# One branch for an expert pair's gate and up products, and one for the two halves of its down product

## The chip, the cores and the metric

The kernel runs on one core of a Trainium2 chip. The metric is the time of one execution on the device in microseconds, the median of the runs; the profile shows one execution, instruction by instruction.

## The reference, cut to what matters

The program computes two stacks of two layers each on 256 tokens of width 1024. The second stack ends each layer with a mixture of 16 experts, and the change lies in these two calls:

```python
def grouped_moe(h, router_w, router_b, w_gate, w_up, w_down):
    # sigmoid router: the best of 4 groups, then the top 2 experts in it
    ...
    for e in range(N_EXPERTS):
        he = jax.nn.silu(t @ w_gate[e]) * (t @ w_up[e])
        y = y + combine[:, e:e + 1] * (he @ w_down[e]).astype(jnp.float32)
```

All of it is float32. An expert has 512 hidden columns, so its gate, up and down weights are 2 MB each.

## The kernel before, in words

`moe` gathers tokens by expert. Experts p and p + 8 form pair p, and the pair shares 128 token slots. How the slots are split between the two is known only at run time: 64 and 64, 96 and 32, or 32 and 96. `gi` holds the split of each pair as 2, 3 or 1, and TensorE loads it into a register (`reg`).

A product of a pair is then written three times, one arm for each split (`products`, L1852 to L1871). `SEG` says how an arm cuts the 128 slots: arm 2 makes two float32 products of 64 columns for each slice of the contraction, arms 3 and 1 make four of 32 columns. `tc.If(gr_ == 2)` (L1865) takes arm 2 or goes on to the inner branch (L1868), which takes arm 3 or arm 1. The arms lie behind one another in TensorE's program: arm 2, arm 3, arm 1, and then the code that follows. So arm 2 jumps over arms 3 and 1 when it ends, arm 3 jumps over arm 1, and arm 1 is reached by two jumps ahead of it. Everything in a branch is scheduled as a unit.

For each of the eight pairs of a call, `pair` (L1873 on) does this on TensorE:

- `products` for the gate (`pg`, 8 slices of the contraction) and `products` for up (`pu`, 8 slices): two branches.
- `gather` (`ga`, L1828): the first half of the next pair's tokens; meanwhile ScalarE takes silu of `pg` (L1879) and VectorE multiplies it by `pu` (L1880).
- four transposes (`tr`, L1886), the second half of `gather`, and then `down(0)` and `down(1)`: two branches of 4 slices each (`pd`), each followed by ScalarE (L1898) and VectorE (L1899), which take the product out of PSUM.
- `back` (`py`, L1906): the rows go back to their tokens, two halves, with `places` (`pw`) for the next pair between them.

In the last pair of a call, `down(1)` is cut in two, with `back(0)` and `back(1)` between the parts, so it has five branches. After the eighth pair stands a loop (L1961) for tokens that found no slot; it ran zero times here.

The weights come in pieces of 1 MB (`piece`, L1620 and L1623, issued by SyncE), 12 for a pair, into a ring of 20 buffers. A piece can be loaded as soon as TensorE has done with the one that held its buffer, 20 pieces earlier.

Of the kernel before, what the change touches and what calls it, by code (L numbers as in the profile page):

```python
# [7 lines left out]
F32 = mybir.dt.float32  # L8
F32R = mybir.dt.float32r
I32 = mybir.dt.int32  # L10
AF = mybir.ActivationFunctionType
OP = mybir.AluOpType
# [5 lines left out]
KD = 8  # L18
# [107 lines left out]
def build(tc, I, out, dump=None, upto=99):  # L126
    nc = tc.nc
    coff, ctot = _const_layout()
    with ExitStack() as ctx:
# [7 lines left out]
        V, S, PE = nc.vector, nc.scalar, nc.tensor  # L137
        mm = PE.matmul
# [31 lines left out]
        def psum(name="ps"):  # L170
            return ps_pool.tile([128, 512], F32, name=name, tag="ps")
# [81 lines left out]
        def mod_buf():  # L253
            return mw["pool"].tile([128, 2048], F32, name="modw", tag="modw", bufs=2)
# [36 lines left out]
        def mod_first(w, b0, bias, dst, dst2, bufs, ahead_=None):  # L291

            rs = []
            for i, buf in enumerate(bufs):
                if i == 3 and ahead_:
                    ahead_()
                r = buf.rearrange("p (k c) -> p k c", k=2)
                nc.sync.dma_start(r, w[i * 256:(i + 1) * 256, b0 * 128:(b0 + 8) * 128].rearrange("(k p) c -> p k c", p=128))
                rs.append(r)
            yield  # L300
            p = psum("modp")
            for k in range(KD):
                for g in range(4):
                    mm(p[g * 32:(g + 1) * 32, :256], cst[:, 0, k, :], rs[k // 2][:, k % 2, g * 256:(g + 1) * 256],
                       start=k == 0, stop=k == KD - 1, skip_group_check=True)
                if k < KD - 1:
                    yield
            yield from mod_out(p, b0, 8, bias, ((0, dst), (1, dst2)))
# [558 lines left out]
        def four(p):  # L867
            return p.rearrange("p (a b) -> p a b", b=128)
# [36 lines left out]
        with ExitStack() as c1:  # L905
# [5 lines left out]
            for x in xs:  # L911
# [3 lines left out]
            scale = mod_first(wm[0], 8, *wm[1:], [mod_buf(), mod_buf(), b4[:, :2048], b4[:, 2048:]],  # L915
                              lambda: load2(0))
            w2t = big("w13r", [128, 2, 2, KD, 128])

            def load2(t):
                for ab in range(2):  # L920
                    nc.sync.dma_start(w2t[:, t, ab], w13[:, ab * FF + t * 128:ab * FF + (t + 1) * 128]
                                      .rearrange("(k p) c -> p k c", p=128))
# [663 lines left out]
        def moe(l, a, op, pre=None, post=None):  # L1586


            with ExitStack() as c1:
# [6 lines left out]
                todo = [(p, e, nm, hf) for p in range(8) for nm in ("exp_w_gate_2", "exp_w_up_2", "exp_w_down_2")  # L1596
                        for hf in range(2) for e in range(2)]
# [71 lines left out]
                w_, r_ = ([f("ew", [128, 4096], F32) for _ in range(n)] for f, n in ((big2, NW), (big, NR)))  # L1669
# [18 lines left out]
                def tm():  # L1688
                    ring_t.append(ring_t.pop(0))
                    return ring_t[-1]  # L1690
# [8 lines left out]
                for tt in range(2):  # L1699
                    V.scalar_tensor_tensor(sc[:, tt], pm[:, 32 + tt * NE:32 + (tt + 1) * NE], rst[:, tt:tt + 1], srow,  # L1700
                                           op0=OP.mult, op1=OP.add)
# [24 lines left out]
                for o, n, d in ((0, 3, 1), (3, 2, 2), (5, 1, 3)):  # L1726
# [44 lines left out]
                                       op0=OP.add, op1=OP.add)  # L1771
# [6 lines left out]
                xg_b = b0_[:, 2 * D:].rearrange("p (k c) -> p k c", k=KD)  # L1778
# [54 lines left out]
                def places(oh, wcol, b):  # L1833
# [5 lines left out]
                    for tt in range(2):  # L1839
# [8 lines left out]
                SEG = {2: ((0, 64, 0), (64, 64, 1)),  # L1848
                       3: ((0, 32, 0), (32, 32, 0), (64, 32, 0), (96, 32, 1)),
                       1: ((0, 32, 0), (32, 32, 1), (64, 32, 1), (96, 32, 1))}  # L1850

                def products(p, x, n_k, w_, gr_, ks=None):  # L1852


                    def arm(n):
                        for k in ks or range(n_k):
                            ws, kp = w_(k)
                            for o, m, e in SEG[n]:
                                mm(p[o:o + m, :], x[:, k, o:o + m], ws[e][kp], start=k == 0, stop=k == n_k - 1,  # L1859
                                   skip_group_check=True)  # L1860
                    if gr_ is None:
                        arm(2)
                        return
                    with tc.issue_after(last[ENG.PE]):
                        with tc.If(gr_ == 2) as c:  # L1865
                            arm(2)
                        with c.Else():
                            with tc.If(gr_ == 3) as c2:  # L1868
                                arm(3)
                            with c2.Else():  # L1870
                                arm(1)  # L1871

                def pair(pl, w_, gr_, nxt=lambda i: None, last_=False):  # L1873

                    pg, pu = psum("pg"), psum("pu")
                    products(pg, xg_b, KD, lambda k: (w_("exp_w_gate_2", k // 4), k % 4), gr_)
                    products(pu, xg_b, KD, lambda k: (w_("exp_w_up_2", k // 4), k % 4), gr_)
                    act = tm()
                    S.activation(act, pg, AF.Silu)  # L1879
                    V.tensor_mul(act, act, pu)  # L1880
                    sw, ohT = pl
                    nxt(0)
                    hT = four(tm())
                    p = psum("tr")
                    for i in range(4):
                        pin(PE.transpose(p[:, i * 128:(i + 1) * 128], act.rearrange("s (j k) -> s k j", k=4)[:, i], ident))  # L1886
                    V.tensor_copy(hT, four(p))
                    nxt(1)
                    dh, dl = b1_[:, :D], b1_[:, D:2 * D]

                    def down(dd, between=None):
                        pd = psum("pd")
                        cs = slice(dd * 512, (dd + 1) * 512)
                        for ks in (range(0, 2), range(2, 4)) if between else (None,):
                            products(pd, hT, 4, lambda k: (w_("exp_w_down_2", k // 2), k % 2 * 2 + dd), gr_, ks)
                            if between and ks[0] == 0:
                                between()
                        S.activation(dh[:, cs], pd, AF.Copy, scale=sw)  # L1898
                        V.scalar_tensor_tensor(dl[:, cs], pd, sw, dh[:, cs].bitcast(F32), op0=OP.mult, op1=OP.subtract)  # L1899

                    def back(d2):
                        py = psum("py")
                        for d in range(2):
                            k = d2 * 2 + d
                            for i, x in enumerate((dh, dl)):
                                pin(mm(py[:, d * T:(d + 1) * T], x[:, k * 128:(k + 1) * 128], ohT,  # L1906
                                       start=i == 0, stop=i == 1))
                        for d in range(2):
                            k = d2 * 2 + d
                            V.scalar_tensor_tensor(XT[:, k], py[:, d * T:(d + 1) * T], g2[:, k:k + 1], XT[:, k],  # L1910
                                                   op0=OP.mult, op1=OP.add)
                    down(0)

                    def half1():
                        back(0)
                        back(1)
                    down(1, half1) if last_ else (down(1), half1())
                    if pre and last_ and gr_ is not None:
                        next(pre, None)
                    if post and last_:  # L1920
                        post(0, tm())
                        post(1, tm())
                    nxt(2)
                    back(2)
                    back(3)
                    if post and last_:
                        post(2, tm())
                        post(3, tm())
# [8 lines left out]
                for p in range(8):  # L1937
                    def nxt(i):
                        if p == 7:
                            return  # L1940
                        if i == 0:
                            gather(ohs[p + 1], 0)
                        elif i == 1:
                            gather(ohs[p + 1], 4)
                        else:
                            pl[p + 1] = places(ohs[p + 1], wt[:, :, p + 1], (p + 1) % 2)
# [14 lines left out]
                with tc.For_i(0, n_extra, 1) as it:  # L1961
# [44 lines left out]
                    def w_(nm, hf):  # L2006
                        if (nm, hf) not in got:
                            b = 2 * len(got)
                            got[nm, hf] = [piece(bufs[2 + (b + e) % 6], I[nm][l][bass.ds(pr_ + 8 * e, 1)]
                                                 .rearrange("o a b -> (o a) b"), nm, hf) for e in range(2)]  # L2010
                        return got[nm, hf]
# [52 lines left out]
```

## Time and profile before

| what | value |
|---|---|
| median of 3 runs | 2053.97 us (2050.93 to 2060.8) |
| profiled execution | 2052.47 us, span 2050.7 us |
| TensorE busy | 1945.3 us, 95% of the span, 14344 matmul records |
| mean granted TensorE clock | 0.979 |
| first call of `moe`, first gate product to last return | 1411.8 to 1639.5 us |
| second call | 1807.5 to 2042 us |

A float32 product appears as two matmul records with a weight load each. PE is TensorE's matmul row, PEld its weight loads, PEldq the instructions that its sequencer handles by itself, such as a branch. The sequencer runs ahead of the array and fills a queue, so a branch stands in the trace before the products ahead of it have run. In the timeline, the number in brackets is how long the engine sat idle before the row. "issue" is a wait for nothing that the profile shows. The queue q8 carries instructions, q1 data.

### The profile page before, as it was taken

To read this page: it belongs to the slowest core of one execution; us is meant where nothing else is said; L and a number is where in the kernel's file an instruction comes from. 1 tells how busy PE (TensorE), PEld (TensorE's weight loads), DVE (VectorE), ACT (ScalarE), POOL (GpSimd) and SP (SyncE) were. 2 spreads that over 40 slices of the span, in tenths; PEclk is the share of its full clock that TensorE was granted. 3 is DMA by queue.
4 is the path that set the end of the run, shared out by engine and by line. 5 is a ranking of instruction groups with operands and counts; after the bars stand their busy time and mean duration, and the time that the engine had idled before them with its cause. 6 is when DMAs were issued, how large, how long until landed. Compare 5 with 4: busy or idle time off the path is not lost. (4 is left out here: it accounts for less than half of the span.)

```text
span 2050.7 us, 34453 instructions
## 1 busy us (share of the span) xinstructions
PE 1945.3 (95%) x14344; PEld 1599.1 (78%) x14344; DVE 1286.9 (63%) x2188; ACT 734.0 (36%) x1075; POOL 64.6 (3%) x60
## 2 busy tenths in 40 slices
PE   6999999999899999999999999998999889889997
PEld 5889899888699989999999999975444488744443
DVE  6357677858797959796798777853223287533222
ACT  4322222245454444445654445441000167500001
POOL 0000000011010010001010010000000010000000
PEclk8999999999999999999999999999999999989999
DMA  8678697734396869776486946468999544879992
GB/s 296 241 252 297 245 325 270 258 103 124 104 335 216 301 172 321 254 261 236 165 299 210 317 150 218 156 233 327 412 416 413 216 149 145 339 321 416 416 411 90
DMA packets 240525, 534.76 MB, mean 261 GB/s; under 512 B 13132, under 2 KB 168128, under 8 KB 206528
## 3 DMA queue, kind: packets, MB, share of 16 engines
q1 hardware_dynamic: 237424, 531.54, 72.0%
q8 instruction: 162, 2.65, 0.5%
q10 hardware_dynamic: 2896, 0.21, 0.2%
q14 instruction: 43, 0.35, 0.0%
HBM read 530.65 MB, written 1.07 MB: 259 GB/s over the span
## 5 line engine op out<-in xcount | busy, mean ns | idle before, releaser
L448 PE MATMUL pa<-hh,whl 128*128 128x258 f32 (+1 forms) x880 | 252.4, 287 | 3.6 <-ACT hh L516 3.6
L450 PE MATMUL pa<-hh,whl 128*128 128x258 f32 (+1 forms) x880 | 249.5, 283 | 4.9 <-DVE whl L419 4.9
L449 PE MATMUL pa<-hl,whl 128*128 128x258 f32 (+1 forms) x880 | 249.4, 283 | 3.3 <-DVE hl L517 3.3
L448 PE MATMUL pb<-hh,whl 128*128 128x258 f32 (+1 forms) x880 | 249.3, 283 | 0.8 <-ACT s L564 0.8
L449 PE MATMUL pb<-hl,whl 128*128 128x258 f32 (+1 forms) x880 | 249.0, 283 | 0.0
L450 PE MATMUL pb<-hh,whl 128*128 128x258 f32 (+1 forms) x880 | 248.9, 283 | 0.0
L324 DVE SCALAR_TENSOR_TENSOR macc<-modw,cst,macc 128x1024 f32<-128x1024 f32 (+1 forms) x182 | 219.9, 1235 | 23.0 <-DMA modw<-in_w_mod_dram 16.1
L418 ACT ACTIVATE whl<-w13r 128x2048 fp32r<-128x2048 f32 x88 | 168.5, 1914 | 179.7 <-PE pb L450 86.3
L419 DVE TENSOR_TENSOR whl<-w13r,whl 128x2048 fp32r<-128x2048 f32 x88 | 201.6, 2291 | 38.5 <-ACT whl L418 38.5
L450 PE MATMUL py<-gh,whl 128*128 128x256 f32 (+1 forms) x704 | 216.7, 308 | 2.7 <-DVE whl L419 2.7
L448 PE MATMUL py<-gh,whl 128*128 128x256 f32 (+1 forms) x704 | 218.4, 310 | 0.1
L449 PE MATMUL py<-gl,whl 128*128 128x256 f32 (+1 forms) x704 | 216.3, 307 | 0.0
L448 PE MATMUL lin<-hh,whl 128*128 128x258 f32 x640 | 188.6, 296 | 5.6 <-ACT hh L516 5.6
L449 PE MATMUL lin<-hl,whl 128*128 128x258 f32 x640 | 181.9, 285 | 3.3 <-DVE hl L517 3.3
L450 PE MATMUL lin<-hh,whl 128*128 128x258 f32 x640 | 181.4, 284 | 0.0
L448 PEld LDWEIGHTS pa<-hh,whl 128*128 128x128 f32 x880 | 166.8, 189 | 11.6 <-ACT hh L516 3.8
L450 PEld LDWEIGHTS pa<-hh,whl 128*128 128x128 f32 x880 | 167.3, 190 | 5.7 <-DVE whl L419 5.3
L449 PEld LDWEIGHTS pa<-hl,whl 128*128 128x128 f32 x880 | 167.7, 191 | 4.1 <-DVE hl L517 3.9
L448 PEld LDWEIGHTS pb<-hh,whl 128*128 128x128 f32 x880 | 166.8, 190 | 1.8 <-ACT s L564 1.0
L450 PEld LDWEIGHTS pb<-hh,whl 128*128 128x128 f32 x880 | 166.9, 190 | 0.4 <-issue 0.4
L449 PEld LDWEIGHTS pb<-hl,whl 128*128 128x128 f32 x880 | 166.9, 190 | 0.0
L418 ACT ACTIVATE whl<-w2r 128x768 fp32r<-128x768 f32 (+3 forms) x80 | 90.7, 1143 | 160.4 <-PE py L450 106.2
(444 smaller groups left out, 3766.7 us busy)
## 6 DMA issues: line engine op xcount, KB each, us to landing
w13r<-in_ffn_w_dram SPq DMA_DIRECT2D x86, 1024.0 KB
modw<-in_w_mod_dram SPq DMA_DIRECT2D x62, 1024.0 KB
ew<-in_exp_w_down_dram SPq DMA_DIRECT2D x54, 1024.0 KB
ew<-in_exp_w_gate_dram SPq DMA_DIRECT2D x54, 1024.0 KB
ew<-in_exp_w_up_dram SPq DMA_DIRECT2D x52, 1024.0 KB
modw<-in_ada_w_dram SPq DMA_DIRECT2D x48, 1024.0 KB
w2r<-in_ffn_w_dram SPq DMA_DIRECT2D x18, 1536.0 KB
w2r<-in_ffn_w_dram SPq DMA_DIRECT2D x12, 1280.0 KB
```

The source lines that it names most:

```text
L324: V.scalar_tensor_tensor(acc[h], x, c, acc[h], op0=OP.mult, op1=OP.add)
L418: S.activation(h, src, AF.Copy)
L419: V.tensor_sub(l, src, h.bitcast(F32))
L448: mm(p, ah, bh, start=start, stop=False)
L449: mm(p, ah, bl, start=False, stop=False)
L450: mm(p, al, bh, start=False, stop=stop)
```

## The change

`products` takes a list of products instead of one, and puts all of them into each arm. Gate and up go into one branch, and the two halves of down into another; the last pair of a call keeps three branches for down. Both PSUM tiles of down are made ahead of the branch, and their readers come after it (`out`). A pair that had four branches has two.

```diff
-                def products(p, x, n_k, w_, gr_, ks=None):
+                def products(x, n_k, gr_, todo):
                     def arm(n):
-                        for k in ks or range(n_k):
-                            ws, kp = w_(k)
-                            for o, m, e in SEG[n]:
-                                mm(p[o:o + m, :], x[:, k, o:o + m], ws[e][kp], start=k == 0, stop=k == n_k - 1,
-                                   skip_group_check=True)
+                        for p, w_, ks in todo:
+                            for k in ks or range(n_k):
+                                ws, kp = w_(k)
+                                for o, m, e in SEG[n]:
+                                    mm(p[o:o + m, :], x[:, k, o:o + m], ws[e][kp], start=k == 0, stop=k == n_k - 1,
+                                       skip_group_check=True)
...
-                    products(pg, xg_b, KD, lambda k: (w_("exp_w_gate_2", k // 4), k % 4), gr_)
-                    products(pu, xg_b, KD, lambda k: (w_("exp_w_up_2", k // 4), k % 4), gr_)
+                    products(xg_b, KD, gr_, [(pg, lambda k: (w_("exp_w_gate_2", k // 4), k % 4), None),
+                                             (pu, lambda k: (w_("exp_w_up_2", k // 4), k % 4), None)])
...
-                    def down(dd, between=None):
-                        pd = psum("pd")
+                    pds = [psum("pd") for _ in range(2)]
+                    def down_of(dd, ks=None):
+                        return pds[dd], lambda k: (w_("exp_w_down_2", k // 2), k % 2 * 2 + dd), ks
+                    def out(dd):
                         cs = slice(dd * 512, (dd + 1) * 512)
-                        for ks in (range(0, 2), range(2, 4)) if between else (None,):
-                            products(pd, hT, 4, lambda k: (w_("exp_w_down_2", k // 2), k % 2 * 2 + dd), gr_, ks)
-                            if between and ks[0] == 0:
-                                between()
-                        S.activation(dh[:, cs], pd, AF.Copy, scale=sw)
-                        V.scalar_tensor_tensor(dl[:, cs], pd, sw, dh[:, cs].bitcast(F32), op0=OP.mult, op1=OP.subtract)
+                        S.activation(dh[:, cs], pds[dd], AF.Copy, scale=sw)
+                        V.scalar_tensor_tensor(dl[:, cs], pds[dd], sw, dh[:, cs].bitcast(F32), op0=OP.mult, op1=OP.subtract)
...
-                    down(0)
...
-                    down(1, half1) if last_ else (down(1), half1())
+                    if last_:
+                        products(hT, 4, gr_, [down_of(0)])
+                        out(0)
+                        products(hT, 4, gr_, [down_of(1, range(0, 2))])
+                        half1()
+                        products(hT, 4, gr_, [down_of(1, range(2, 4))])
+                        out(1)
+                    else:
+                        products(hT, 4, gr_, [down_of(0), down_of(1)])
+                        out(0)
+                        out(1)
+                        half1()
```

## Rows read from the trace of the kernel before

**Rows 1.** Busy time by stretch: window, its length, engines, PEclk, DMA share, GB/s.

```profile
1440.00:1468.00 28.00, 28.00 (x157) 13.54 (x158) 8.11 (x19) 1.97 (x3) 0.00 (x0) 1.00 1.01 415
1900.00:1920.00 20.00, 17.73 (x148) 7.72 (x144) 3.01 (x5) 1.28 (x2) 0.00 (x0) 0.91 1.02 412
```

**Rows 2.** Chain that ended last, second pair of the second call: start, us, what.

```profile
1837.09 7.07 PE pg L1859 x63
1844.16 6.87 PE pu L1859 x64
1851.02 1.98 PE ga L1828 x16
...
1853.48 1.79 PE ga L1828 x16
1855.27 7.00 PE pd L1859 x64
```

**Rows 3.** Timeline, TensorE's idle times inside the pairs, both calls.

```profile
1511.43 2.02 PE L1828 MATMUL ga<-oh,nx 128*128 128x128 f32 x16 [1.66 <-DVE tm L1880]
...
1596.99 1.27 PE L1828 MATMUL ga<-oh,nx 128*128 128x128 f32 x10 [1.82 <-issue]
...
1618.88 1.51 PE L1859 MATMUL pu<-ew,nx 128*64 128x512 f32 x6 [0.91 <-PE pg L1859]
...
1837.09 0.63 PE L1859 MATMUL pg<-ew,nx 128*32 128x512 f32 x4 [0.85 <-issue]
...
1903.95 4.48 PE L1859 MATMUL pu<-ew,nx 128*32 128x512 f32 x24 [2.27 <-issue]
...
1968.57 1.16 PE L1828 MATMUL ga<-oh,nx 128*128 128x128 f32 x9 [1.45 <-issue]
...
1991.42 1.08 PE L1859 MATMUL pu<-ew,nx 128*64 128x512 f32 x4 [1.95 <-issue]
```

**Rows 4.** Branches of L1865: duration ns min/median/max; all, then single ones.

```profile
L1865 PEldq COMPARE_BRANCH  x116: 63/188/6082, 1411.2 to 2034.3; - x116
...
L1865 PEldq COMPARE_BRANCH  x1: 5932/5932/5932, 1505.3 to 1505.3; - x1
...
L1865 PEldq COMPARE_BRANCH  x1: 5042/5042/5042, 1613.5 to 1613.5; - x1
...
L1865 PEldq COMPARE_BRANCH  x1: 6082/6082/6082, 1985.0 to 1985.0; - x1
...
L1865 PEldq COMPARE_BRANCH  x1: 2897/2897/2897, 1994.0 to 1994.0; - x1
```

**Rows 5.** DMA queues of the whole span: the instruction queue, packets, MB, share.

```profile
q8 instruction: 162, 2.65, 0.5%
```

**Rows 6.** DMA queues: instructions, 1411.8 to 1637 (first call); all queues, 1636 to 1643.

```profile
q8 instruction: 34, 0.56, 1.0%
...
DMA packets 1, 0.02 MB, mean 2 GB/s; under 512 B 0, under 2 KB 0, under 8 KB 0
```

**Rows 7.** The branch over the loop, end of the first call.

```profile
L1961 PEldq COMPARE_BRANCH  x1: 3325/3325/3325, 1639.7 to 1639.7; - x1
```

**Rows 8.** Gate products: all of them; in the timeline one in arm 2, one in arm 1.

```profile
L1859 PE MATMUL pg<-ew,nx x640: 589/592/643, 1411.8 to 2019.0; 128*64 128x512 f32 x96, 128*32 128x512 f32 x64
...
1411.83 7.09 PE L1859 MATMUL pg<-ew,nx 128*64 128x512 f32 x32
...
1807.50 7.07 PE L1859 MATMUL pg<-ew,nx 128*32 128x512 f32 x64
```

**Rows 9.** A branch of L1865 ahead of a gate product in arm 1.

```profile
L1865 PEldq COMPARE_BRANCH  x1: 207/207/207, 1834.6 to 1834.6; - x1
```

**Rows 10.** Weight issues after the first gate products; busy time after the last weights.

```profile
1415.51 4.24 SPq L1623 DMA_DIRECT2D ew<-in_exp_w_down_dram  x4
...
1812.89 2.70 SPq L1623 DMA_DIRECT2D ew<-in_exp_w_down_dram  x4
...
2012.00:2028.00 16.00, 15.14 (x73) 5.38 (x71) 3.59 (x10) 0.60 (x1) 0.00 (x0) 1.00 0.01 3
```

## The prediction

> **What bounds the kernel now.** I read the profile from the whole to the one pair: busy time by stretch, the chain that ended last, TensorE's idle times, the branches, the instruction queue, and last the weights. [...] The chain runs through TensorE without a break: 7.1 us gate, 6.9 up, 2.0 and 1.8 gather, 7.0 down [rows 2]. Between gate and up, and between the halves of down, where branches stand, no idle time shows here. So what a branch costs has to be looked for in the seven places where TensorE stood: 1.66 + 1.82 + 0.91 + 0.85 + 2.27 + 1.45 + 1.95 = 10.9 us over both calls [rows 3]. Three of the seven stand ahead of or inside a gather, which reads no weights.
>
> The branches explain them. Their median is 0.19 us, but single ones last 5.9, 5.0 and 6.1 us [rows 4], and TensorE's 1.66, 0.91 and 1.95 us of idle time follow these three. The long ones wait for code. The instruction queue brings 162 packets of 2.65 MB / 162 = 16.4 KB [rows 5]. A pair's code, counted from the kernel, is 3 x (64 + 128 + 128) = 960 loads and matmuls of products (gate, up, down; an arm 2 of gate is 32 matmuls, so 64 instructions, an arm 1 twice that [rows 8]), and about 150 for the rest: some 1,110. The first call's eight pairs brought 34 packets [rows 6], so a packet holds about 8 x 1,110 / 34 = 260 instructions; I call it a block and count with 256. All arms are fetched, run or not.
>
> Three things follow from the rows.
>
> - One block ahead is held, not two. The branch over the loop at 1639.7 us skips more than a block and took 3.3 us [rows 7], and the only DMA packet from 1636 to 1643, 0.02 MB, is one of code [rows 6]: the data queues were at rest.
> - In a pair, with the DMA engines full, a block is usable 5.8 us after the sequencer entered the one before: it got out of the 6.08 us branch at 1985.0 + 6.1 = 1991.1, and out of the next long one at 1994.0 + 2.9 = 1996.9 [rows 4].
> - TensorE's queue hides about 4.2 us of such a wait in arm 2: 5.93 - 1.66 = 4.3, 5.04 - 0.91 = 4.1, 6.08 - 1.95 = 4.1 [rows 3, 4].
>
> [...]
>
> **The change part by part.** What it removes is small: two branches of four in 14 pairs and one of five in the last pair of each call, at 0.2 us of sequencer time each [rows 4], all under the queue: 0. Code shrinks by about 8 of 1,110 instructions a pair, so about as many blocks are fetched. What matters is how far a branch now jumps. Arm 2 of gate skipped 256 instructions, one block, and landed in the block that was already asked for. Arm 2 of gate and up together skips 512, two blocks, so the target is never the block at hand.
>
> (a) Gate and up in arm 2. The 640 gate matmuls are 12 x 32 + 4 x 64 [rows 8]: 12 of 16 pairs take arm 2 (all of the first call, four of the second); the other four go through two branches ahead of the arm and none behind it, so arm 1. In the last pair of each call the data queues are at rest and the wait is about the 3.3 us of [rows 7], less than the queue hides. The other 10 wait 5.85 and hide 4.2: 10 x 1.65 = 16.5 us. In the first pair of the first call the sequencer crosses into a block some 20 instructions, 2 us, before the arm ends, and if skipped blocks are fetched in order, a second wait is added: 0 to 5.8 - 2 = 3.8, I take 2.
>
> (b) Behind the landing the queue is empty and the next block has only been asked for. If fewer than about 90 instructions are left in the landing block, TensorE runs them (32 of a gather take 1.98 us, 0.062 each [rows 2]) and stands again. The stop at 1596.99, after one load and one product of the gather [rows 3], fixes a block's edge. Counted from it, with 8 instructions less for each pair, the seven landings of the first call leave 229, 148, 78, 8, 194, 124 and 54 instructions, and the three of the second 178, 108 and 38. The short ones give 5.8 - 0.062 x n = 1.0 + 5.3 + 2.5 + 3.4 = 12.2 us. (An edge that is 50 places off gives 8 to 16.)
>
> (c) Down. The merged branch jumps 256 as one gate branch does now, and lands in the next block. Some will wait as these did, 0.9 to 1.95 us [rows 3]: three of 14 at 1.5, 4.5 us; bounds 0 and 14 x 1.95 = 27.
>
> (d) Arm 1, four pairs. Its jumps lie ahead of the arm: 128 + 256 instructions, 1.5 blocks instead of 0.75. By the same count three of the four land two blocks on. The branch stands at 1834.6 [rows 9] and the product follows about 1 us later (1.5 us less a gap of 0.85 in this pair [rows 3]), so only 1 us is hidden: 4.8 us twice, 2.5 for the first pair, whose data queues are at rest, and 1 for the fourth: 13 us. Bounds: 0, and 4 x 5.8 = 23.
>
> (e) The clock. [...] After 1.95 us, four matmuls took 1.08 [rows 3], full speed. Six of the new gaps are longer than 2.27 us: 6 x 1.7 = 10 us. Bounds 0 and 20.
>
> (f) What stands now, 10.9 and 1.7 us, is replaced: -12.6.
>
> At nothing I cost the readers. ScalarE's silu of `pg` may start only when up is done, if the branch signals at its end: 0.6 us more ahead of the multiplication, under the 2.0 us of gather [rows 2]; without a gather, in two last pairs, 1.2 us. The first half of down is taken out later; that lies under the second half's 3.5 us. If it waited for the branch's end, about 1.5 us would be bare in 14 pairs, 21 us. What I see speaks against it: the signals lie inside an arm, since the first weight issue of a gate came 3.7 us after its start in arm 2 and 5.4 in arm 1, before the 7.1 were over [rows 8, 10]. In arm 1 the gate's buffers come free some 3.5 us later when both share a branch. Behind that wait, on SyncE's queue, stand only weights that are not yet due: from 2012 to 2028 us the data queues move nothing (share 0.01) [rows 10], so the last pieces are ready over 16 us early.
>
> Sum: 16.5 + 2 + 12.2 + 4.5 + 13 + 10 - 12.6 = 45.6 us. Against the profiled execution's own 2052.47 us that is 2098 us; the median of the runs is 1.5 us above it, less than anything here can tell.
>
> **The rivals.** *The long jump is free, faster.* If TensorE holds more than two blocks, or fetches the target while the arm runs, twice as long an arm gives twice the time to do so, and with half the branches the present stalls go: 2052.5 - 10.9 - 1.7 = 2040 us. It decides from a wait under 4.2 us in (a), for then (b) starts with code at hand. For it: most branches of L1865 are short, 0.19 us in the median [rows 4]. Against it: the 3.3 us of [rows 7], where two blocks on was not there although the code before it had run for some microseconds. [...]
>
> *The queue hides it, no change.* Behind 13.7 us of matmuls the queue is always full, so (a) costs 10 x 0 to 0.5 us, and if (b) and (d) are half of what I count, without slow clocks, they take the place of the old 12.6: 2052 to 2062, within 10 us of now. Against it: three long branches give the same 4.2 us of cover.
>
> *Skipped blocks are fetched one by one and weights come late, slower still.* Where the block ahead isn't in when a jump starts, two waits follow each other. This adds up to 5.8 us in some three jumps, and with down's upper bound about 20 us: 2118.
>
> **How the numbers follow.** Long jump paid, as summed: 0.82. Paid and stacked: 0.06. Free: 0.06. Hidden: 0.06, half of which is within 0.5%. Half a per cent, 10 us, is about what a measurement of this kernel can tell from no change. The range takes (a) and (d) with half of the rest from below, 16.5 + 13 - 12.6 = 17, so 2070, and the stacked case from above, 2118; outside lie the free and the hidden case. Faster 0.06, within 0.5% 0.04, slower 0.90.
>
> **What would show it.** In the branches of L1865, about 58 fewer rows, and in the pairs of arm 2 a long one, 5 to 6 us, behind nearly every gate and up product; TensorE idle 1.5 to 2 us at the first gather of each, and ahead of a gate product in arm 1. Packets of the instruction queue stay near 160. Idle time in the pairs grows from 10.9 to 50 us or so, and granted clocks below 1.00 show in more stretches. The prediction is wrong if the branches behind gate and up stay under 4 us, if the gaps end at weights, or if ScalarE's read of `pd` sets the way back.

## The result, and the profile after

The changed kernel takes 2141.65 us in the median (2135.36 to 2145.23, 4 runs) against 2052.8 us of the kernel before beside it: 1.042 times as long, with an interval of 1.038 to 1.046. The sign was forecast, the size was not: 2098 us were expected and 2070 to 2118 allowed, so the loss is 89 us instead of 46.

The profiled execution took 2145.23 us, span 2143.5 (before 2050.7). Of the 92.8 us between the spans, 48.7 lie in the first call of `moe`, 5.5 between the calls, 37.7 from the second call to the end and 0.9 ahead of the first. These are the busy times by stretch: first call, what lies between, second call to the end.

```profile
1412.70:1689.10 276.40, 238.39 (x1195) 114.20 (x1194) 63.57 (x132) 17.96 (x28) 0.00 (x0) 0.93 0.76 298
1689.10:1856.00 166.90, 145.67 (x1069) 131.21 (x1070) 115.66 (x243) 103.57 (x148) 7.19 (x7) 0.91 0.59 212
1856.00:2143.50 287.50, 245.23 (x1632) 116.28 (x1632) 65.56 (x138) 17.95 (x28) 0.00 (x0) 0.92 0.71 285
```

Two things grew in the first stretch. TensorE is busy 238 of 276 us, so it stands for 38; and the granted clock is 0.93, where the pairs of before showed 1.00 [rows 1]. (The same three stretches of before: 227.7 us at a granted clock of 1.00, 161.4 at 0.95, 249.8 at 0.97.) The DMA share fell to 0.76, and none of TensorE's idle times in the two calls ends at a DMA, so weights aren't what is waited for.

The branches come first, with duration in ns as min/median/max. All of L1866, then single ones: behind gate and up in arm 2, behind down in arm 2, ahead of gate in arm 1 (there the inner branch, L1869, jumps), and behind gate and up of the last pair, whose data queues are at rest.

```profile
L1866 PEldq COMPARE_BRANCH  x64: 63/207/6643, 1412.0 to 2127.1; - x64
...
L1866 PEldq COMPARE_BRANCH  x1: 5952/5952/5952, 1422.2 to 1422.2; - x1
...
L1866 PEldq COMPARE_BRANCH  x1: 6020/6020/6020, 1612.7 to 1612.7; - x1
...
L1869 PEldq COMPARE_BRANCH  x1: 5608/5608/5608, 1895.2 to 1895.2; - x1
...
L1866 PEldq COMPARE_BRANCH  x1: 3401/3401/3401, 1671.1 to 1671.1; - x1
```

All ten jumps behind gate and up that are taken while weights stream last 5.8 to 6.6 us, where before three branches of L1865 lasted 5 us or more in both calls together [rows 4]. The instruction queue still brings 162 packets of 2.65 MB, as in [rows 5].

TensorE's idle times, from the timeline (the number in brackets): two landings of a jump on a gather, behind the second of which TensorE waits once more inside the gather, and two gate products in arm 1.

```profile
1431.03 1.22 PE L1828 MATMUL ga<-oh,nx 128*128 128x128 f32 x4 [4.39 <-issue]
...
1534.71 0.82 PE L1828 MATMUL ga<-oh,nx 128*128 128x128 f32 x5 [2.08 <-issue]
1541.10 2.71 PE L1828 MATMUL ga<-oh,nx 128*128 128x128 f32 x11 [5.57 <-issue]
...
1901.02 5.24 PE L1860 MATMUL pg<-ew,nx 128*32 128x512 f32 x28 [4.49 <-issue]
...
1971.46 1.93 PE L1860 MATMUL pg<-ew,nx 128*32 128x512 f32 x8 [5.30 <-issue]
```

Not all of the first one, 4.39 us, is a wait for code. The branch at 1422.2 ends at 1428.2, and between it and the first product of the gather TensorE's sequencer loads the splits of four pairs into registers (`reg`), which takes it to 1431.0, 2.8 us:

```profile
L1941 PEldq TENSOR_LOAD <-gi x4: 297/304/313, 1428.2 to 1430.3; - x4
```

At the other nine landings behind gate and up the stand is the branch less 4.4 us each time, as 6.02 - 1.64 at 1465 and 6.64 - 2.26 at 1643.

Grouped over both calls, with the idle time and its releasers behind the last bar:

```profile
L1860 PE MATMUL pg<-ew,nx 128*64 128x512 f32 (+1 forms) x640 | 130.5, 671 | 13.4 <-issue 13.4
...
L1828 PE MATMUL ga<-oh,nx 128*128 128x128 f32 x482 | 68.3, 300 | 28.9 <-issue 16.7 <-DVE tm L1881 9.4 <-DVE left L1808 2.7
...
L1907 PE MATMUL py<-dd 128*128 128x256 f32 x255 | 47.8, 325 | 29.7 <-DVE dd L1900 23.1 <-ACT dd L1899 5.5 <-issue 1.1
```

The first two rows are the waits for code that were forecast: 13.4 us ahead of gate products, and 28.9 - 2.7 = 26.2 at gathers, 2.8 of them the register loads. (For 9.4 us of the latter the view names VectorE's multiplication of L1881; but that ended ahead of the landing, as it did ahead of the 1.66 us of [rows 3], and the branch that ends each of these waits is the 6 us one.) The third row was not forecast: 23.1 us ahead of `py`, released by VectorE's L1900, the subtraction that takes down out of PSUM. The chain that ended last shows how, in the first 64/64 pair of the second call: start, us, what.

```profile
2030.76 0.68 PE py L1907 x4
2031.43 0.03 issue
2031.46 1.13 DVE XT L1911 x3
...
2032.64 0.47 DVE XT L1911
2033.12 0.07 DVE sw L1842
2033.18 0.33 DVE dd L1844
2033.51 0.67 DVE dd L1900
...
2034.22 1.38 PE py L1907 x7
2035.60 8.35 PE pg L1860 x32
```

The chain leaves TensorE. After the first half of the way back, VectorE does the four adds into `XT` and the next pair's copies (L1842, L1844), and only then the second half's subtraction, on which the second half of the way back waits. In the kernel before, both subtractions stand ahead of the adds, as in its first pair of the second call:

```profile
1833.78 0.75 DVE L1899 SCALAR_TENSOR_TENSOR dd<-pd,sw,dd 128x512 fp32r<-128x512 f32 x1 [2.71 <-ACT dd L1898]
...
1834.45 1.65 DVE L1910 SCALAR_TENSOR_TENSOR XT<-py,mod_a,XT 128x256 f32<-128x256 f32 x4
```

`back(0)` and `back(1)` need the first half of down alone; with both readers behind the branch, VectorE's order has the adds between them, although the source still calls `out(1)` ahead of `half1()`. TensorE stands 1.60 us in each of the 14 pairs that aren't last, 22.4 us. And the gate product that follows takes 8.35 us instead of 7.09 [rows 8]: the granted clock is 0.84 from 2035.6 to 2043.95 us, and 0.50 from 2036 to 2038.

### The profile page after: what moved, and what is told of

Its sections match the earlier page's. It is cut to its first block, busy times and chain, and to the rows that moved or that the text cites. A ratio compares the mean times of both kernels' runs of the same rounds, so it can differ in the third digit from the quotient of the medians.

```text
span 2143.5 us, 34381 instructions
## 1 busy us (share of the span) xinstructions
PE 1980.4 (92%) x14344; PEld 1615.6 (75%) x14344; DVE 1288.5 (60%) x2188; ACT 734.4 (34%) x1075; POOL 64.3 (3%) x60
## 3 DMA queue, kind: packets, MB, share of 16 engines
q8 instruction: 162, 2.65, 0.5%
HBM read 530.65 MB, written 1.07 MB: 248 GB/s over the span
## 5 line engine op out<-in xcount | busy, mean ns | idle before, releaser
L450 PE MATMUL pa<-hh,whl 128*128 128x258 f32 (+1 forms) x880 | 249.8, 284 | 4.5 <-DVE whl L419 4.5
L1881 DVE TENSOR_TENSOR tm<-tm,pu 128x512 f32<-128x512 f32 x16 | 11.0, 688 | 238.9 <-PE pu L1860 238.9
```

Of the source, the lines that this page charges most:

```text
L450: mm(p, al, bh, start=False, stop=stop)
```

## The experiments

In the table, *stands* is the sum of TensorE's idle times over 0.25 us in both calls, from the timeline, less the 6.3 us at the ends of the two calls that every kernel here has. *Clock* is what the span lost to the granted clock: (1 - mean granted clock) x span of the profiled execution, so 0.021 x 2050.7 = 43 us before. It is that of one execution: over the 15 runs of the kernel before beside one of these experiments the mean clock lay between 0.973 and 0.980, 41 to 56 us.

| kernel | median us | ratio to before, interval | stands us | clock us |
|---|---|---|---|---|
| before | 2052.8 | | 10.9 | 43 |
| changed | 2141.65 | 1.042 (1.038 to 1.046) | 67 | 81 |
| gate and up shared alone | 2102.41 | 1.025 (1.022 to 1.027) | 43 | 63 |
| down shared alone | 2084.33 | 1.016 (1.013 to 1.019) | 28 | 54 |
| changed, order in part | 2123.03 | 1.034 (1.031 to 1.037) | 60 | 66 |
| changed, order of before | 2110.63 | 1.026 (1.025 to 1.028) | 54 | 63 |
| changed, without arm 3 | 2077.58 | 1.012 (1.009 to 1.014) | 24 | 58 |
| both undone | 2045.15 | 0.995 (0.993 to 0.996) | 1.7 | 47 |
| before, without arm 3 | 2043.9 | 0.994 (0.992 to 0.996) | 0 | 47 |
| order of before, no reload | 2056.12 | 1.000 (0.999 to 1.002) | 11 | 51 |
| before, wide arm 3 | 2044.19 | 0.994 (0.992 to 0.996) | 0 | 47 |
| before, inner quarters apart | 2084.11 | 1.014 (1.012 to 1.016) | 0 | 35 |
| before, three parts | 2151.69 | 1.047 (1.045 to 1.049) | 0 | 43 |
| order of before, three parts | 2165.47 | 1.054 (1.052 to 1.056) | 14 | 45 |

Each ratio is to runs of the kernel before beside it, whose medians lie between 2052.8 and 2057.5 us. But for the last three, whose products themselves got longer, stands and clock together give each span to within 6 us: for the changed kernel 67 - 10.9 + 81 - 43 = 94 against 92.8.

The theory had three parts: a jump past two blocks of code waits for a fetch, VectorE's order bares 1.6 us in a pair, and the clock falls after such stands. Its rivals: weights or the shared branch as such; one of the two products alone.

**One half of the change at a time.** The first kernel shares the branch of gate and up; down goes branch by branch, each with its reader behind it.

```diff
-                        products(hT, 4, gr_, [down_of(0), down_of(1)])
+                        products(hT, 4, gr_, [down_of(0)])
                         out(0)
+                        products(hT, 4, gr_, [down_of(1)])
                         out(1)
                         half1()
```

The second shares the branch of down, and gate and up have one each.

```diff
-                    products(xg_b, KD, gr_, [(pg, lambda k: (w_("exp_w_gate_2", k // 4), k % 4), None),
-                                             (pu, lambda k: (w_("exp_w_up_2", k // 4), k % 4), None)])
+                    products(xg_b, KD, gr_, [(pg, lambda k: (w_("exp_w_gate_2", k // 4), k % 4), None)])
+                    products(xg_b, KD, gr_, [(pu, lambda k: (w_("exp_w_up_2", k // 4), k % 4), None)])
```

> Gate and up share a branch; down keeps its two, each with its readers behind it. Theory (waits for code, a VectorE order, and a slow clock that follows the gaps): the code part alone is left. 10 branches of 5 to 6 us behind gate and up, TensorE's gaps at the gathers and ahead of arm 1 together about 39 us as in the changed kernel, and no 1.6 us between the two halves of the way back; with the stands of before that are left (some 3 us) less its 10.9, and half of some 25 us of half clock: 2052.8 + 32 + 12, 2090 to 2105 us. Rival (the halves of down or late weights do it all, the long jump is cheap): 2055 to 2065.

> Gate and up keep two branches; the halves of down share one. Theory: VectorE's order is as in the changed kernel, so TensorE stands 1.6 us between the halves of the way back in 14 pairs, 22 us, with no 5.9 us branch behind more pairs than before; the gaps bring some slow clock, 5 to 15 us: 2080 to 2090 us. Rival (the readers of down cost nothing, as the prediction had it, and the whole loss is the long jump of gate and up): 2052 to 2058.

They took 2102.41 and 2084.33 us, both inside what the theory gave. Their losses, 48 and 30 us, make up 78 of the 89. First the gathers and the way back of the one with gate and up, grouped over both calls:

```profile
L1828 PE MATMUL ga<-oh,nx 128*128 128x128 f32 x512 | 70.3, 295 | 33.9 <-issue 17.9 <-DVE tm L1881 10.6 <-DVE left L1808 5.5
L1907 PE MATMUL py<-dd 128*128 128x256 f32 x255 | 39.5, 296 | 3.9 <-ACT dd L1899 2.2 <-issue 0.9 <-DVE dd L1900 0.8
```

And the same of the one with down:

```profile
L1828 PE MATMUL ga<-oh,nx 128*128 128x128 f32 x512 | 68.5, 291 | 8.9 <-DVE left L1808 5.5 <-DVE tm L1881 3.4
L1907 PE MATMUL py<-dd 128*128 128x256 f32 x255 | 47.1, 322 | 27.0 <-DVE dd L1900 23.1 <-ACT dd L1899 2.1 <-issue 1.8
```

Each half has its own cause. With gate and up shared, TensorE stands at the gathers (33.9, of which 5.5 are the starts of the two calls) and waits 0.8 us for L1900; with down shared it is 3.4 and 23.1. Of down's 23.1, 14 x 1.6 = 22.4 are the pairs and 0.8 the ends of the calls.

**VectorE's order.** The changed kernel, with the second subtraction first.

```diff
                         out(0)
-                        out(1)
-                        half1()
+                        with tc.issue_after(out(1).ins):
+                            half1()
+                            nxt(2)
...
-                    nxt(2)
+                    if last_:
+                        nxt(2)
```

> The changed kernel with VectorE's order as before the change: the second half's subtraction stands ahead of the adds into XT and the next pair's copies. Branches are as in the changed kernel. Theory: the 14 gaps of 1.6 us go, 22 us, and with them a part of the slow clock, 5 to 15 us: 2105 to 2115 us. Rival one (the slow clock follows the long waits for code alone): 2119. Rival two (the order is only where the wait shows, and it moves elsewhere): 2135 to 2142.

At 2123.03 us it gained 18.6, less than the theory's 27 to 37 and nearer the first rival. The timeline of a pair says why.

```profile
1510.72 0.69 ACT L1899 ACTIVATE dd<-pd,sw 128x512 fp32r<-128x512 f32 x1 [2.76 <-PE pd L1860]
...
1512.42 0.43 DVE L1783 TENSOR_TENSOR oh<-c_iota,slot 128x256 f32<-128x256 f32 x1 [3.67 <-PE pw L1840]
1512.77 0.75 DVE L1900 SCALAR_TENSOR_TENSOR dd<-pd,sw,dd 128x512 fp32r<-128x512 f32 x1
...
1513.57 1.10 PE L1907 MATMUL py<-dd 128*128 128x256 f32 x7 [1.06 <-DVE dd L1900]
```

ScalarE was done at 1511.41, but a one-hot for a later pair (L1783) now stood ahead of the subtraction, and it waits until TensorE has read its buffer (`pw`). The stand shrank from 1.60 to 1.06 us. So I put the one-hot behind the subtraction too, which is the order of before (`sub` holds that subtraction):

```diff
+                        with tc.issue_after(sub[0]) if sub else ExitStack():
-                        ohs[p + 1] = onehot(p + 1)
+                            ohs[p + 1] = onehot(p + 1)
```

> The changed kernel with VectorE's order of before in full. In the earlier run with the subtraction ahead of the adds, the 14 gaps went from 1.60 to 1.06 us, because a one-hot that waits for TensorE's read of its buffer still stood ahead of the subtraction; here it stands behind it too. Theory: the 14 x 1.06 = 14.8 us left go as well, with 3 to 8 us of slow clock: 2100 to 2106 us, near the 2102 of gate and up alone. Rival (the gap belongs to the shared branch of down, whose first half is signalled late, and not to the order): 2119 to 2123.

It took 2110.63 us, 31 less than the changed kernel. In the same pair the way back has no stand:

```profile
1505.61 0.69 ACT L1900 ACTIVATE dd<-pd,sw 128x512 fp32r<-128x512 f32 x1 [2.76 <-PE pd L1861]
1506.34 0.75 DVE L1901 SCALAR_TENSOR_TENSOR dd<-pd,sw,dd 128x512 fp32r<-128x512 f32 x1 [2.69 <-ACT dd L1900]
...
1507.00 1.65 DVE L1912 SCALAR_TENSOR_TENSOR XT<-py,mod_a,XT 128x256 f32<-128x256 f32 x4
1507.03 1.21 PE L1908 MATMUL py<-dd 128*128 128x256 f32 x8
```

The rival is out: the wait belonged to the order, not to a shared branch. The time lies 5 us above what I expected, and its trace has 4 us more of code waits ahead of arm 1 (17.2 us, after 13.4) and a new stand of 3.5 us among transposes, 5.8 us behind a landing.

**The length of the jump.** The arm for a 96/32 split is left out, first of the changed kernel, then of the kernel before, then of the changed kernel with VectorE's order of before. No pair of this input takes that arm.

```diff
-                            with tc.If(gr_ == 3) as c2:
-                                arm(3)
-                            with c2.Else():
-                                arm(1)
+                            arm(1)
```

> The changed kernel without the arm for a 96/32 split, which no pair of this input takes: arm 2 of gate and up jumps 256 instructions instead of 512, and down 128 instead of 256; arm 1 jumps over 128 instead of 384. Theory: the landing is the block at hand or the one ahead, so the gaps of 26 us at the gathers and 13 us ahead of arm 1 shrink to under 10 us; the 14 x 1.6 us of VectorE's order stay, with some slow clock: 2075 to 2095 us. Rival (a merged branch costs its wait whatever its length, or the weights are late): 2130 to 2142.

> The kernel before without the arm for a 96/32 split, which no pair of this input takes: arm 2 jumps 128 instructions instead of 256, arm 1 over 64 instead of 192. Theory: no branch in the pairs waits over the 4.2 us that the queue hides, so the 10.9 us of stands go and a little slow clock: 2042 to 2047 us. Rival (those stands come from something else in the pair): 2052 to 2056.

> The changed kernel with both causes undone: without the arm for a 96/32 split, which no pair takes here, and with VectorE's order of before. Theory: of the 88 us nothing is left, since shared branches as such cost nothing: 2042 to 2050 us, level with the kernel before without that arm. Rival (there is a third cause in the sharing, such as readers that wait for a branch's end): 2058 to 2070.

All three came out as the theory had it: 2077.58, 2043.9 and 2045.15 us. The branches of the first, which still shares them but jumps 256 instructions instead of 512, and its stands:

```profile
L1866 PEldq COMPARE_BRANCH  x64: 63/179/2497, 1412.3 to 2065.4; - x64
```

```profile
L1828 PE MATMUL ga<-oh,nx 128*128 128x128 f32 x512 | 67.7, 289 | 6.7 <-DVE left L1808 5.5 <-DVE tm L1878 0.9 <-issue 0.3
L1904 PE MATMUL py<-dd 128*128 128x256 f32 x255 | 47.6, 325 | 25.2 <-DVE dd L1897 23.1 <-ACT dd L1896 2.1
```

No branch lasts over 2.5 us, the gathers stand for 1.2 us beyond the calls' starts (0.9 of it behind the four register loads), and VectorE's 23.1 us are left whole. In the kernel before without the arm, which jumps 128, no branch of L1865 exceeds 1.07 us and the 10.9 us of [rows 3] are gone. And with both causes undone the shared branches take 2045.15 us, level with that, so there is no third cause.

To leave the arm out also makes the program shorter, 137 packets of code instead of 162. That alone isn't what helps: three kernels of the table have 150 packets and jumps of 192 instructions and no stand in a pair, and a fourth has 150 as well, but jumps of 384, and stands for 14 us.

The two kernels without arm 3, with the change's order on VectorE and with that of before, also show what stands of 1.6 us do to the clock. The same 1143 matmuls of the first call, from its first gate product to the last pair's transposes, with the change's order first:

```profile
1412.90:1643.00 230.10, 217.18 (x1143) 101.38 (x1142) 58.55 (x124) 14.62 (x23) 0.00 (x0) 0.97 0.89 357
...
1410.40:1621.00 210.60, 209.46 (x1143) 98.70 (x1142) 56.92 (x123) 14.62 (x23) 0.00 (x0) 1.00 0.96 389
```

In the first the granted clock falls as eight of the 14 stands ahead of `py` end, four in each call, and is 0.97 in this stretch; in the second it is 1.00 up to the last pair's transposes. Over the whole of the two calls it is 0.97 and 0.96 in the one, 0.99 and 0.98 in the other, and TensorE is busy 467.9 us in the one and 454.3 in the other.

**What the fetch competes with.** The changed kernel with the order of before, in which no weight is loaded into a buffer a second time (its result is therefore not the program's).

```diff
-                                wpiece[todo[n + j]] = piece(bufs[(n + j) % RING], I[nm][l, p + 8 * e], nm, hf, ks)
+                                wpiece[todo[n + j]] = rows4(bufs[(n + j) % RING]) if again else piece(
+                                    bufs[(n + j) % RING], I[nm][l, p + 8 * e], nm, hf, ks)
```

> The changed kernel with VectorE's order of before, and no weight loaded into a buffer a second time: after the first 20 pieces of a call every product reads what the buffer holds, so the data queues are nearly at rest while the pairs run (the weights of most pairs are then those of others). Theory: a code block that has the DMA engines for itself arrives after some 3.3 us, as the loop's branch did, less than the 4.2 us that TensorE's queue hides: the branches behind gate and up fall from 6 to about 3.3 us, the gaps of 26 us behind them to under 5, those ahead of arm 1 from 14 to some 9, with less slow clock: 2060 to 2075 us. Rival (a fetch takes its 5.9 us whatever the data queues do, or TensorE's sequencer itself needs it): 2105 to 2112.

It took 2056.12 us, 54 us less, a little better than expected. The branches, all and one behind gate and up:

```profile
L1868 PEldq COMPARE_BRANCH  x64: 63/210/3823, 1413.1 to 2043.0; - x64
...
L1868 PEldq COMPARE_BRANCH  x1: 3303/3303/3303, 1423.2 to 1423.2; - x1
```

With a DMA share of 0.01 in a stretch that had 0.92, the same jumps last 3.3 to 3.8 us. That is under the 4.2 us that TensorE's queue hides behind an arm 2, and over what it hides ahead of an arm 1: of the 11 us of stands left, 2.6 + 2.8 + 2.9 stand ahead of gate products in arm 1, and 1.7 + 1.4 at two gathers, the first of which follows the register loads.

**A kernel that beats both.** If jumps of half a block cost nothing, the uneven arms are worth shortening. Three ways that keep all splits: the two outer quarters shared by both uneven arms, with a branch for the inner ones; three parts in place of four; and a 96/32 arm that multiplies all 128 places by the first expert and then the last 32 by the second.

The first:

```diff
-                       3: ((0, 32, 0), (32, 32, 0), (64, 32, 0), (96, 32, 1)),
-                       1: ((0, 32, 0), (32, 32, 1), (64, 32, 1), (96, 32, 1))}
+                       0: ((0, 32, 0), (96, 32, 1)),
+                       3: ((32, 32, 0), (64, 32, 0)),
+                       1: ((32, 32, 1), (64, 32, 1))}
...
                         with c.Else():
+                            arm(0)
                             with tc.If(gr_ == 3) as c2:
```

The second, on the kernel before and, as a run of its own, on the changed kernel with VectorE's order of before:

```diff
+                       3: ((0, 64, 0), (64, 32, 0), (96, 32, 1)),
+                       1: ((0, 32, 0), (32, 32, 1), (64, 64, 1))}
```

The third:

```diff
                     def arm(n):
+                        if n == 3 and ks is None:
+                            for o, m, e in ((0, 128, 0), (96, 32, 1)):
+                                for k in range(n_k):
+                                    ws, kp = w_(k)
+                                    mm(p[o:o + m, :], x[:, k, o:o + m], ws[e][kp], start=k == 0, stop=k == n_k - 1,
+                                       skip_group_check=True)
+                            return
```

> The kernel before, with the arms for 96/32 and 32/96 made one for the two outer quarters and a branch for the two inner ones alone: all splits are still computed, and arm 2 jumps 192 instructions of a product instead of 256. Theory: a jump that is three quarters of a block lands in the block at hand more often, so a part of the 10.9 us goes: 2043 to 2052 us. Rival (one more branch for each product of a 32/96 pair costs more than that): 2055 to 2062.

> The kernel before with the uneven splits in three parts instead of four: 96/32 as 64 + 32 and 32, 32/96 as 32 and 32 + 64. All splits are still computed; an uneven arm has 96 instructions instead of 128, so arm 2 jumps 192 instead of 256, and arm 1 over 160 instead of 192. Theory: as in the run with the two inner quarters apart, whose first call had no stand, the long branches go: 2042 to 2048 us, faster than both kernels. Rival (a 64-column part beside two of 32 columns takes longer than four of 32, as two quarters at a time did): 2050 to 2075.

> The changed kernel with VectorE's order of before and the uneven splits in three parts: arm 2 of gate and up jumps 384 instructions, a block and a half, instead of 512; arm 1 over 320 instead of 384. Theory (one block ahead is at hand): about half of the landings lie two blocks on, so about half of the code waits of the run with 512 are left: 2070 to 2090 us. Rival (any jump beyond the 256 waits alike): 2100 to 2112.

> The kernel before, where the 96/32 arm multiplies all 128 places by the first expert and then the last 32 by the second, in runs of one width each: 64 instructions instead of 128 (the last pair's halved product of down keeps its four quarters). All splits are still computed, and arm 1 stays as it is, four quarters of 32; no pair of this input takes the shortened arm, so its own speed is not in the time. Arm 2 jumps 192 instructions instead of 256, arm 1 over 128 instead of 192. Theory: as in the first calls of the two runs whose uneven arms were changed, no pair stands for code: 2042 to 2048 us, faster than both kernels. Rival (192 still lands two blocks on in a few pairs): 2048 to 2056.

The first two took 2084.11 and 2151.69 us, far over what I expected, and three parts under shared branches 2165.47. The first calls, which have only 64/64 pairs, did as the theory had it: no stand with jumps of 192 instructions (225 us from the first gate product to the last return, as without the arm, and 228 before), and four stands at gathers, 0.9 to 2.2 us, with jumps of 384. What failed is the second call, whose four 32/96 pairs got longer without a stand. The gate product of such a pair took 7.07 us in four quarters [rows 8]; here it is in three parts.

```profile
1807.77 15.95 PE L1859 MATMUL pg<-ew,nx 128*32 128x512 f32 x48
```

So 48 matmuls of mixed width take 15.95 us, at a granted clock of 0.98 from 1801.8 to 1900 us, where 64 of 32 columns take 7.07. With two quarters at a time the four gate products were busy for 49.0 us together, 12.3 each. The uneven arms have to stay as they are where they run. The wide arm leaves them so, and shortens only the one that is jumped over: 2044.19 us, 0.994 times the kernel before (0.992 to 0.996), and no stand in a pair. It beats both kernels. A 96/32 pair would run that arm; what it then costs isn't measured.

## Why the prediction was right in sign and wrong in size

**The long jumps: right in sum, not in every part.** Terms (a) to (d) came to 48 us, and the trace after has 44.6.

- (a): 20.1 us at ten landings behind gate and up, where 18.5 were forecast. The ten waits forecast at 16.5 measure 17.3 without the register loads. The 2 us for a second wait in the first pair were luck: what stands there is the four register loads, 2.8 us, and no second fetch.
- (b): 6.6 us (0.62 + 5.57 + 0.40), where 12.2 were forecast, at least 8. The landing with 8 instructions left stood 5.57 us, and that with 78 left 0.62. The one with 54 left, forecast at 2.5, did not stand: the gather behind it took 3.55 us at a granted clock of 0.55 instead of 2.02 [rows 3], which covers 1.5 of it. With VectorE's order of before, all four short landings stand, for 0.81 + 5.63 + 2.47 + 3.48 = 12.4 us, so the count from one known edge was sound.
- (c): 4.5 us ahead of `py`, in three of 14 pairs, as forecast.
- (d): 3.27 + 4.49 + 0.34 + 5.30 = 13.4 us ahead of or in gate products of arm 1, where 13 were forecast.

The block's length and the 5.8 us held; the queue hid 4.4 us instead of 4.2. Code kept TensorE standing for 42 us in the changed kernel, where gate and up jump 512 instructions, for 0.3 without arm 3, where they jump 256 (10.9 before, with two such jumps in a pair), and not at all where they jump 128 or 192. How much code TensorE holds no run shows; the one block ahead was my estimate from the 3.3 us of [rows 7].

**The readers "at nothing": wrong.** This is the first step that failed. The working looked at when `pd` is signalled, and that was right: ScalarE takes the first half out while the second runs. It even priced what would follow if the way back were bared, 1.5 us in 14 pairs, 21 us, but hung it on ScalarE's wait for the branch and ruled it out there. What wasn't asked is the order on VectorE: which instructions the second reader would stand behind once both readers follow one branch. That cost 22.4 us of stands. The trace of before can't show an order that is yet to come, but it has the price: the four adds and the copies keep VectorE for about 2 us, as the chain above shows again with 1.13 + 0.47 + 0.07 + 0.33.

**The clock: mechanism right, size not.** This is the second. Term (e) gave 1.7 us to each of six gaps over 2.27 us, 10 us, bounds 0 and 20. The rows give 81 - 43 = 38 us, most of it in the two calls: 0.07 x 276.4 + 0.08 x 287.5 - 0.03 x 249.8 = 35. (Between the calls the clock was 0.91, but with both causes undone it was 0.92 there too.) TensorE's busy time agrees: for the same 14344 matmul records it grew from 1945.3 to 1980.4 us, by 35. What failed is the choice that only gaps longer than 2.27 us count, drawn from a single stand of 1.95 us that no lower clock followed. In the pairs of the changed kernel the granted clock falls to 0.50 13 times (once before), and ten of these falls lie in, or within 2 us behind, a stand of 1.6 us ahead of `py`. Nor does any run show 1.7 us as the price of every such gap: behind the 2.27 us one 24 matmuls took 4.48 us [rows 3], at a granted clock of 0.62, where 64 take 7.07 [rows 8] and so 24 some 2.65; that is 1.8 us, 11 for six gaps. In the changed kernel the 64 gate matmuls behind 3.27, 4.49 and 5.30 us took 7.08, 9.10 and 9.71 us.

**The sum.** Forecast 48.2 + 10 - 12.6 = 45.6. Measured 44.6 of code and register loads, 22.4 of order and 38 of clock, less the 10.9 that stood before: 94, for 92.8 of span.

**The rivals.** The free jump and the hidden one are out, since every jump of 512 instructions that was taken under load lasted 5.8 us or more and left TensorE standing for 1.4 us or more. The stacked case is out too: no branch of the changed kernel lasted over 6.64 us, and down stood for 4.5 us, not 27. Its time was passed for other reasons, and it was added up short besides: three waits of 5.8 us, and 27 us of down instead of 4.5, are 40 us more and not 20, which would be 2138. (The lower bound, 17 us, likewise lacks the half of the rest that it names, 14 us.)

**Left open.** Why a given stand is followed by the lower clock and another isn't (eight of 14 alike, without arm 3) was not settled; the account takes the clock's cost as the rows show it. Why the last short landing of (b) stood 0.40 us in the changed kernel, and 3.48 with VectorE's order of before, is open as well.

## What to carry to other kernels

What a branch cost here went by how much code its end jumps over (5.8 to 6.6 us over 512 instructions, at most 2.5 over 256 without arm 3) and by what else the DMA engines did (3.3 to 3.8 us over 512 at a DMA share of 0.01), not by its median of 0.2 us: to merge two doubled the jump, and to shorten an arm that never runs was worth more (0.6%) than to save branches. When readers are moved behind a shared block, follow each engine's order past the move, and ask what now stands between two instructions that stood together. Price an idle time on TensorE with the clock that follows it: here 56 us more of stands brought 38 us of slow clock.

## What the runs showed of the hardware that I had not expected

- Matmuls of 32 columns were cheap only where all four quarters follow one another: 64 of them take 7.07 us [rows 8], 12.3 when two quarters at a time are addressed, and 48 of mixed 32 and 64 columns 15.95 us.
- A block of code that had the DMA engines nearly to itself (share 0.01) kept a branch waiting for 3.3 to 3.8 us, beside the weights for 5.8 to 6.6 us, though it is 16.4 KB in either case.
- Stands of 1.6 us, with none longer in the pairs, were enough to bring the lower clock: it followed eight of 14 of them, and TensorE was busy 13.6 us longer in the two calls (467.9 after 454.3).
- Four loads of registers took TensorE's sequencer 2.8 us. In the kernel before, where products were still queued (the loads begin at 1424.5 us), TensorE did not stand for them; behind the jump of 512 instructions, with the queue empty, it stood for all of it.
